# Strassen products for the up projections of two feed-forward blocks, and a down phase of its own

## The chip, the cores and the metric

The kernel runs on one core of one Trainium2 chip. The metric is the device time of one execution in microseconds. The engines are TensorE (PE, with its weight loads PEld), VectorE (DVE), ScalarE (ACT), GpSimd (POOL) and SyncE (SP), which here only issues transfers.

## The reference

Three blocks follow each other on x, 1024 tokens of 1024 channels. Block 2 and the first parts of blocks 1 and 3 (mixers and attention) are left alone. What the change touches are the feed-forward parts of blocks 1 and 3, with D_FF = 2816:

```python
h = rmsnorm(x, ffn_norm_g[l])
up = causal_depthwise_conv(h @ w_up[l], conv_w[l], conv_b[l])
a, bgate = jnp.split(up, [D_FF], axis=-1)
x = x + (jax.nn.silu(a) * bgate) @ w_down[l]
...
gate, up = jnp.split(h @ w_gate_up, 2, axis=-1)
return (jax.nn.silu(gate) * up) @ w_down
```

The convolution of block 1 is over three tokens, per channel. In block 3 the result is added to ALPHA times the residual, and a layer norm follows.

## The kernel before

Tiles hold 128 channels by 512 tokens; the tokens come as two halves. A matmul is made of three: each operand is split into a high part (rounded to float32r by ScalarE, line 324) and a low part (the rest, by GpSimd or VectorE, line 330), and high by high, high by low and low by high are summed in one PSUM bank (line 344). The function `split` writes this pair, and `w_load` does it for weights: a raw tile of 512 KB is loaded by SP (`w_dma`, line 359), and whi and wlo of 128 by 1024 are made of it. The weights of the whole program lie in one array, in the order of use, so a change of that order is a change in `_weights`.

The program is written as generators. The main one issues the matmuls and, right behind a product, what evicts it; side tasks are taken in between by a `Driver` that counts estimated time. What comes out is a fixed order on every engine, and semaphores between engines; each engine takes its own queue in order.

A feed-forward part (`ffn`) has 22 chunks (NFF). Chunk c is one tile of 128 gate channels (w = 0) and one of 128 value channels (w = 1): two weight tiles, two halves, eight k-tiles. Chunks 0 and 1 are done by `first_quad`, the others by `gemm_a` into banks named up; `evac` makes g of them, and `g_split` splits g into ghi and glo for the down product. After every second chunk `down` adds the products of two chunks of g with their rows of w_down to the 16 tiles X of the residual, in banks named dn. The last four chunks are added at the end.

In block 1, `evac` multiplies by the norm's row R into a tile u, and does the convolution on it: ScalarE's Identity with scale and bias, then two steps on VectorE, then Silu (w = 0) or the product with the gate (w = 1). The two tokens that the second half needs of the first are kept in a tile carry. In block 3, `evac` is Silu for w = 0 and a product for w = 1.

Of the kernel before, what the change touches and what calls it, by code (L numbers as in the profile page):

```python
# [39 lines left out]
def _weights(a):  # L40
# [9 lines left out]
    def ffn(up, down):  # L50
# [48 lines left out]


# [198 lines left out]
class Kernel:  # L299
    def __init__(self, tc, ins, outs, blocks=(1, 2, 3)):  # L300
        self.tc, self.nc, self.a, self.o = tc, tc.nc, ins, outs
        self.blocks = blocks
        self.drv = Driver()
        self.wn = 0
        self.wl, self.raws = [], []
        self.wi = self.wd = 0

# [35 lines left out]
    def mm(self, out, lhsT, rhs, start, stop):  # L343
        self.nc.tensor.matmul(out=out, lhsT=lhsT, rhs=rhs, start=start, stop=stop)  # L344
# [17 lines left out]

    def w_load(self):

        if self.wi >= self.a["wall"].shape[0]:
            return
# [20 lines left out]
    def w_retire(self, n):  # L387
        self.live -= n
        while len(self.wl) + self.live < 4 and self.wi < self.a["wall"].shape[0]:
            self.w_load()  # L390
# [110 lines left out]
    def build(self):  # L501
# [4 lines left out]
        with ExitStack() as ctx:  # L506
# [5 lines left out]
            self.hp = e(name="h", bufs=66)  # L512
# [10 lines left out]
            self.x2d = self.dp.tile([8, 128, S], F32, name="x2d")  # L523
            self.yd = self.dp.tile([8, 128, S], F32, name="yd")
# [16 lines left out]
    def first_quad(self, evac):  # L541

        ws = self.w_take(4)
        for half in range(2):
            self.drv.force(self.hs[half])
            pend = []
            for g in (0, 2):
                pss = [self.bank("fq") for _ in range(2)]
                yield from self.gemm_q(pss, ws[g:g + 2], half)
# [195 lines left out]
    def block1(self):  # L745
# [290 lines left out]
        def o_evac(j, half, ps):  # L1036
            self.tt(X[j][half], ps, X[j][half], ALU.add)
            sq = self.h("sq")
            self.act(sq, X[j][half], AF.Square)
            self.add_acc(accx, half, sq, nc.vector)  # L1040

        new_hs, new_rs = [None, None], [None, None]

        def done(half):
            new_hs[half] = drv.add(self.gen_split(half, lambda c: X[c][half],
                                                  lambda c: self.v("ffn_norm_g", c), H3), 500.0)
            new_rs[half] = drv.add(self.gen_rms(accx[half], half, D, 1e-6), 4800.0)
# [3 lines left out]
        self.H, self.hs, self.rs = H3, new_hs, new_rs  # L1051
# [10 lines left out]
        def evac(c, w, half, ps, up, G):  # L1062
            ch = c + NFF * w
            u = up.tile([128, HF + 2], F32, tag="u", bufs=4, name="u")
# [59 lines left out]
        yield from self.ffn(evac, add_last, done2, last)  # L1124
        self.H, self.hs, self.rs = H4, [iter(()), iter(())], rs

    def g_split(self, up, t, c):
        if c == NFF - 1:
            hi, lo = self.h("ghi", F32R), self.h("glo", F32R)
        else:  # L1130
            hi = up.tile([128, HF], F32R, tag="g", bufs=12, name="ghi")
            lo = up.tile([128, HF], F32R, tag="g", bufs=12, name="glo")
        self.split(hi, lo, t)
        return hi, lo

    def ffn(self, evac, add_last, done, by_half):

        X, G = self.X, {}
        with self.tc.tile_pool(name="ffn", bufs=4) as up:
            def down(i, ws, order, ev):  # L1140
                for j, half in order:
# [1017 lines left out]
```

## Time and profile before

| what | value |
|---|---|
| median of 3 runs | 3219.21 us (3215.55 to 3222.81) |
| profiled execution | 3218.23 us |
| its span, first to last instruction | 3216.4 us |
| mean granted TensorE clock | 0.966 |
| PE, DVE, ACT, POOL busy | 95%, 50%, 37%, 35% |
| HBM traffic | 161.06 MB read, 22.28 MB written |

The page counts an engine as busy while an instruction of its own runs; shares are means over parts of the program with different limits, so the same figures by stretch of time matter more. The feed-forward part of block 1 lies between about 445 and 1170 us of the span, that of block 3 between about 2440 and 3190.

### The profile page before, as it was taken

The numbers are of one execution on the slowest core, as the hardware profiler recorded it, in microseconds if no ns is written. First come the engines' busy times: TensorE is split into PE (matmuls) and PEld (weight loads), VectorE is DVE, ScalarE is ACT, GpSimd is POOL, SyncE is SP. The second block draws the span as 40 slices with busy tenths as digits, with TensorE's granted clock in tenths as the row PEclk, the third lists the DMA queues.
The fourth block names the chain that finished last, engine by engine and source line by source line (L and its number), as shares of the span: only waits on it lengthen the run. The fifth ranks groups of instructions, "written<-read, shape, count | busy, mean of one in ns | idle before, by whom it ended". The sixth has DMA issues, their size and how long they took to land.

```text
span 3216.4 us, 40756 instructions
## 1 busy us (share of the span) xinstructions
PE 3047.1 (95%) x15656; PEld 2592.4 (81%) x15656; DVE 1620.9 (50%) x3172; ACT 1179.0 (37%) x2276; POOL 1130.5 (35%) x899
## 2 busy tenths in 40 slices
PE   8999999999999989889998989988799999999997
PEld 7897788888888877868897779877688888888886
DVE  6443354444444469966646664666757112211216
ACT  4232232222222253566673356644435111111113
POOL 4314423333232365952214342234323323223321
PEclk9999999999999999989998989999799999999997
DMA  4101121111111112122113322100212111111111
GB/s 155 38 16 55 63 66 53 53 50 47 48 47 46 53 55 72 49 95 59 48 36 109 110 95 65 42 20 22 78 53 66 53 53 53 50 43 53 47 45 53
DMA packets 80306, 185.98 MB, mean 58 GB/s; under 512 B 15856, under 2 KB 27760, under 8 KB 80112
## 3 DMA queue, kind: packets, MB, share of 16 engines
q1 hardware_dynamic: 79824, 183.08, 17.7%
q8 instruction: 124, 2.03, 0.3%
q14 instruction: 70, 0.57, 0.1%
q10 hardware_dynamic: 288, 0.30, 0.0%
HBM read 161.06 MB, written 22.28 MB: 57 GB/s over the span
## 4 chain that ended last, share of the span: by engine, by line
PE 42%; DVE 8%; ACT 3%; issue 1%; DMA 0%; POOL 0%; ACTq 0%; DVEq 0%; SPq 0%; POOLq 0%
PE up L344 14%; PE dn L344 7%; PE op L344 5%; PE qk L344 3%; PE fq L344 2%; DVE f L1869 2%; PE o L344 2%; PE zp L344 1%; PE vp L344 1%; DVE pt L1885 1%; PE s L344 1%; PE sbo L344 1%; PE swo L344 1%; PE pt L1442 1%; PE ln L344 1%
## 5 line engine op out<-in xcount | busy, mean ns | idle before, releaser
L330 POOL TENSOR_TENSOR wlo<-raw,whi 128x1024 fp32r<-128x1024 f32 x240 | 580.2, 2435 | 720.0 <-ACT whi L324 704.3
L344 PE MATMUL up<-hlo,whi 128*128 128x512 f32 x1280 | 498.0, 389 | 0.0
L344 PE MATMUL up<-hhi,wlo 128*128 128x512 f32 x1280 | 498.0, 389 | 0.0
L344 PE MATMUL up<-hhi,whi 128*128 128x512 f32 x1280 | 497.9, 389 | 0.0
L324 ACT ACTIVATE whi<-raw 128x1024 fp32r<-128x1024 f32 x240 | 243.4, 1050 | 430.9 <-PE dn L344 292.2
L330 DVE TENSOR_TENSOR X<-dn,X 128x512 f32<-128x512 f32 (+1 forms) x328 | 219.4, 676 | 181.6 <-PE dn L344 181.4
L344 PE MATMUL dn<-ghi,whi 128*128 128x512 f32 (+1 forms) x736 | 283.0, 384 | 0.0
L344 PE MATMUL dn<-glo,whi 128*128 128x512 f32 (+1 forms) x736 | 282.4, 384 | 0.0
L344 PE MATMUL dn<-ghi,wlo 128*128 128x512 f32 (+1 forms) x736 | 282.2, 383 | 0.0
L344 PEld LDWEIGHTS up<-hlo,whi 128*128 128x128 f32 x1280 | 240.3, 188 | 50.0
L344 PEld LDWEIGHTS up<-hhi,whi 128*128 128x128 f32 x1280 | 240.3, 188 | 49.9
L344 PEld LDWEIGHTS up<-hhi,wlo 128*128 128x128 f32 x1280 | 240.3, 188 | 49.9
L330 DVE TENSOR_TENSOR gate<-up,gate 128x512 f32<-128x512 f32 x40 | 27.7, 692 | 406.7 <-PE up L344 406.7
L327 DVE SCALAR_TENSOR_TENSOR cv<-u,vec,cv 128x512 f32<-128x512 f32 x176 | 132.3, 752 | 138.0 <-ACT cv L324 61.1
L330 POOL TENSOR_TENSOR glo<-gate,ghi 128x512 fp32r<-128x512 f32 x44 | 56.9, 1292 | 335.3 <-ACT ghi L324 317.8
L344 PE MATMUL qk<-hhi,whi 128*128 128x512 f32 x384 | 163.3, 425 | 7.8 <-ACT hhi L324 7.1
L344 PEld LDWEIGHTS dn<-glo,whi 128*128 128x128 f32 x736 | 139.4, 189 | 28.3
L344 PEld LDWEIGHTS dn<-ghi,whi 128*128 128x128 f32 x736 | 139.4, 189 | 28.3
L344 PEld LDWEIGHTS dn<-ghi,wlo 128*128 128x128 f32 x736 | 139.3, 189 | 28.3
L344 PE MATMUL op<-hhi,wlo 128*128 128x512 f32 x384 | 154.2, 402 | 4.0 <-POOL wlo L330 4.0
L344 PE MATMUL op<-hhi,whi 128*128 128x512 f32 x384 | 156.3, 407 | 0.0
L344 PE MATMUL qk<-hlo,whi 128*128 128x512 f32 x384 | 154.5, 402 | 1.2 <-DVE hlo L327 1.2
(374 smaller groups left out, 6771.5 us busy)
## 6 DMA issues: line engine op xcount, KB each, us to landing
raw<-in_wall SPq DMA_DIRECT2D x240, 512.0 KB, 3.5
x2d<-X SPq DMA_DIRECT2D x32, 256.0 KB, 2.0
X<-x2d SPq DMA_DIRECT2D x32, 256.0 KB, 4.2
x<-in_xT SPq DMA_DIRECT2D x16, 256.0 KB, 5.9
X<-in_xT SPq DMA_DIRECT2D x16, 256.0 KB, 6.2
T<-in_rpbx SPq DMA_DIRECT2D x8, 448.0 KB, 3.9
yd<-ys SPq DMA_DIRECT2D x56, 64.0 KB, 1.6
c2d<-z SPq DMA_DIRECT2D x8, 256.0 KB, 4.3
```

Source lines behind the costliest of these rows:

```text
L324: self.nc.scalar.activation(out=out, in_=in_, func=func, bias=bias, scale=scale, **kw)
L327: self.nc.vector.scalar_tensor_tensor(out=out, in0=in0, scalar=s, in1=in1, op0=op0, op1=op1)
L330: (eng or self.nc.vector).tensor_tensor(out=out, in0=in0, in1=in1, op=op)
L344: self.nc.tensor.matmul(out=out, lhsT=lhsT, rhs=rhs, start=start, stop=stop)
L1442: nc.tensor.transpose(ps[:, 128 * b:128 * b + 128], pr[:, 128 * b:128 * b + 128], self.ident)
L1869: nc.vector.tensor_tensor_scan(out=rev, data0=rev, data1=rev, initial=carry, op0=ALU.mult, op1=ALU.bypass)
L1885: nc.vector.tensor_copy(out=pt[:, 0:w], in_=pst[:, 0:w])
```

## The change

Chunks 2 to 21 of both feed-forward parts are computed by seven products in place of eight. A chunk's weights are the two by two quarters A11, A12 (gate channels, first and second half of k) and A21, A22 (value channels), h the quarters B11 to B22 (k by half of the tokens). With S1 = A21 + A22, S2 = S1 - A11, S3 = A11 - A21, S4 = A12 - S2 and T1 = B12 - B11, T2 = B22 - T1, T3 = B22 - B12, T4 = B21 - T2, the products are P1 = A11 B11, P2 = A12 B21, P3 = S4 B22, P4 = A22 T4, P5 = S1 T1, P6 = S2 T2, P7 = S3 T3. They are summed in three banks named p1, p2 and p3 and in tiles e1, v1 and v2. In the code, X[c][0] and X[c][1] become the T in `gen_t`, once a block; `s_steps` gives six steps that make a chunk's S from its two raw tiles while the chunk before is multiplied, and `strassen` calls them between the products. A quarter is a pair shi, slo; A1 holds A11 and A12, S24 holds S2 and S4, as pairs whi, wlo.

For this, h is multiplied by the norm's row before it is split (`gen_h` in place of `gen_split` and `gen_rms`). X is overwritten by the T, so the residual goes to DRAM (x2d) before and comes back for the down phase; g goes to DRAM (gd) as it is made, and is loaded and split in a down phase after all chunks (`g_load`). The convolution's tile t lies in PSUM, the carry is copied by VectorE, and half of a chunk's evictions (`later`) are issued in the next chunk. The weights' order in the array follows.

```diff
-        u(0), u(1)
-        for i in range(1, NFF // 2 - 1):
-            u(2 * i)
-            out.extend([dn[2 * i - 2], dn[2 * i - 1]])
-            u(2 * i + 1)
-        u(NFF - 2), u(NFF - 1)
+        for c in range(NFF):
+            u(c)
+        out.extend(dn[:NFF - 4])
...
+S_TILES = ((36, 76), (178, 218))
...
-            self.hp = e(name="h", bufs=66)
+            self.hp = e(name="h", bufs=64)
...
-            self.tt(X[j][half], ps, X[j][half], ALU.add)
+            x = X[j][half]
+            self.tt(x, ps, x, ALU.add)
+            nc.sync.dma_start(out=self.x2d[j][:, HF * half:HF * half + HF], in_=x)
...
+            for c in range(8):
+                x = X[c][half]
+                hi, lo = self.h("hhi", F32R), self.h("hlo", F32R)
+                H3[0][c][half], H3[1][c][half] = hi, lo
+                self.stt(x, x, self.v("ffn_norm_g", c), row, ALU.mult, ALU.mult)
+                self.split(hi, lo, x, eng=nc.vector if c % 2 else None)
+                yield 0.0, 900.0
...
+        def put(c, w, half, ps, add):
+            u = UT[c, w, half] = self.up.tile([128, HF + 2], F32, tag="u", bufs=4, name="u")
+            if add is None:
+                self.act(u[:, 2:HF + 2], ps, AF.Copy)
+            else:
+                self.tt(u[:, 2:HF + 2], ps, add, ALU.add)
+        def conv(c, w, half):
+            ch, u = c + NFF * w, UT.pop((c, w, half))
             if half == 0:
-                nc.gpsimd.memset(u[:, 0:2], 0.0)
+                nc.vector.memset(u[:, 0:2], 0.0)
+                U[c, w] = self.small(2, "carry")
+                nc.vector.tensor_copy(out=U[c, w], in_=u[:, HF:HF + 2])
             else:
-                nc.gpsimd.tensor_copy(out=u[:, 0:2], in_=U.pop((c, w)))
-            self.tt(u[:, 2:HF + 2], ps, R[half], ALU.mult)
-            if half == 0:
-                U[c, w] = self.small(2, "carry")
-                nc.gpsimd.tensor_copy(out=U[c, w], in_=u[:, HF:HF + 2])
-            t = self.h("cv")
+                nc.vector.tensor_copy(out=u[:, 0:2], in_=U.pop((c, w)))
+            t = self.pt.tile([128, 512], F32, tag="t", name="t")
             self.act(t, u[:, 2:HF + 2], AF.Identity, bias=self.v("conv_b", ch), scale=self.v("conv_w2", ch))
             self.stt(t, u[:, 1:HF + 1], self.v("conv_w1", ch), t, ALU.mult, ALU.add)
             self.stt(t, u[:, 0:HF], self.v("conv_w0", ch), t, ALU.mult, ALU.add)
             if w == 0:
-                self.act(t, t, AF.Silu)
-                G[c, half] = t
+                A[c, half] = self.h("a")
+                self.act(A[c, half], t, AF.Silu)
             else:
-                self.tt(t, G[c, half], t, ALU.mult)
-                G[c, half] = self.g_split(up, t, c)
+                g = self.h("g")
+                self.tt(g, t, A.pop((c, half)), ALU.mult)
+                self.g_out(c, half, g)
+        def evac(c, w, half, ps):
+            put(c, w, half, ps, None)
+            conv(c, w, half)
...
+        def half(i, k, x):
+            T[i][0][k], T[i][1][k] = self.h("thi", F32R), self.h("tlo", F32R)
+            self.split(T[i][0][k], T[i][1][k], x, eng=P if k == 3 else V)
+        for k in range(4):
+            x11, x12 = X[k]
+            self.tt(x11, x12, x11, ALU.subtract)
+            half(1, k, x11)
+        yield
+        for k in range(4):
+            x11, x22 = X[k][0], X[k + 4][1]
+            self.tt(x11, x22, x11, ALU.subtract)
+            half(2, k, x11)
+        for k in range(4):
+            x12, x22 = X[k][1], X[k + 4][1]
+            self.tt(x12, x22, x12, ALU.subtract)
+            half(3, k, x12)
+        for k in range(4):
+            x11, x21 = X[k][0], X[k + 4][0]
+            self.tt(x21, x21, x11, ALU.subtract)
+            half(4, k, x21)
...
+        def quarter(src):
+            hi, lo = (self.up.tile([128, 512], F32R, tag="e", bufs=12, name=x) for x in ("shi", "slo"))
+            self.split(hi, lo, src)
+            return hi, lo
+        def whole(src):
+            hi = self.wp.tile([128, 1024], F32R, tag="whi", bufs=4, name="whi")
+            lo = self.wp.tile([128, 1024], F32R, tag="wlo", bufs=4, name="wlo")
+            self.split(hi, lo, src)
+            return hi, lo
+        L, R = slice(0, 512), slice(512, 1024)
+        ra = rb = None
+        def s0():
+            nonlocal ra, rb
+            ra, rb = self.raws[0:2]
+            self.raws = self.raws[2:]
+            self.wi += 2
+            st["A22"] = quarter(rb[:, R])
+        def s1():
+            self.tt(rb[:, R], rb[:, L], rb[:, R], ALU.add, P)
+            self.tt(rb[:, L], ra[:, L], rb[:, L], ALU.subtract, P)
+        def s2():
+            st["S1"] = quarter(rb[:, R])
+            st["S3"] = quarter(rb[:, L])
+        def s3():
+            st["A1"] = whole(ra)
+        def s4():
+            self.tt(ra[:, L], rb[:, R], ra[:, L], ALU.subtract, P)
+            self.tt(ra[:, R], ra[:, R], ra[:, L], ALU.subtract, P)
+        def s5():
+            st["S24"] = whole(ra)
+        return [s0, s1, s2, s3, s4, s5]
...
+            b1, b2, b3 = (self.bank(x) for x in ("p1", "p2", "p3"))
+            def p6():
+                yield from prod(b2, cur["S24"], 0, T[2], True)
+            def p1():
+                yield from prod(b1, cur["A1"], 0, B11, True)
+            if n == 0:
+                yield from p1()
+                yield from prod(b3, cur["S1"], 0, T[1], True)
+                yield from p6()
+            else:
+                yield from p6()
+                step()
+                yield from p1()
+            e1, v1 = self.h("e1"), self.h("v1")
+            self.act(e1, b1, AF.Copy)
+            self.tt(v1, b2, e1, ALU.add)
+            step()
+            for f in left[0]:
+                f()
+            if n > 0:
+                yield from prod(b3, cur["S1"], 0, T[1], True)
+            step()
+            yield from prod(b2, cur["S3"], 0, T[3], False)
+            v2 = self.h("v2")
+            self.tt(v2, b2, e1, ALU.add)
+            put(c, 1, 1, b3, v2)
+            step()
+            yield from prod(b1, cur["A1"], 512, B21, False)
+            put(c, 0, 0, b1, None)
+            for f in left[1]:
+                f()
+            step()
+            yield from prod(b2, cur["A22"], 0, T[4], False)
+            put(c, 1, 0, b2, e1)
+            for f in left[2]:
+                f()
+            step()
+            while steps:
+                step()
+            if n + 2 < n_all:
+                self.s_dma(n + 2)
+            elif n + 2 == n_all:
+                self.w_dma()
+                self.w_dma()
+            else:
+                tail()
+            yield from prod(b3, cur["S24"], 512, B22, False)
+            put(c, 0, 1, b3, v1)
+            left = later(c)
+            cur = nxt
...
+                if g == 0:
+                    for f in steps[0:3]:
+                        f()
...
+            def g_load(c, half, own):
+                x = self.h("gx")
+                nc.sync.dma_start(out=x, in_=self.gd[c][:, HF * half:HF * half + HF])
+                hi, lo = ((self.up.tile([128, 512], F32R, tag="e", bufs=12, name=y) if own else self.h(y, F32R))
+                          for y in ("ghi", "glo"))
+                self.split(hi, lo, x, eng=nc.vector if half else None)
+                G[c, half] = hi, lo
...
+            def tail():
+                del self.stops[0]
+                for a in g_group(0):
+                    g_load(*a)
+                for j in range(8):
                     for half in range(2):
-                        for w in range(2):
-                            ps = self.bank("up")
-                            yield from self.gemm_a(ps, ws[w], half)
-                            evac(c, w, half, ps, up, G)
-                    self.w_retire(2)
-                    if c == 2 * i and i < NFF // 2 - 1:
-                        ws = self.w_take(2)
-                        yield from down(i - 1, ws, every, add)
-                        self.w_retire(2)
+                        X[j][half] = self.h("X")
+                        nc.sync.dma_start(out=X[j][half], in_=self.x2d[j][:, HF * half:HF * half + HF])
+                self.w_load()
...
+        def put(c, w, half, ps, add):
+            if w and half:
+                B[c] = self.pt.tile([128, 512], F32, tag="t", name="t")
+                self.tt(B[c], ps, add, ALU.add)
+            elif w:
+                self.tt(ps, ps, add, ALU.add)
+                gate(c, 0, ps)
+            else:
+                a = A[c, half] = self.h("a")
+                if add is not None:
+                    self.tt(a, ps, add, ALU.add)
+                self.act(a, ps if add is None else a, AF.Silu)
+        def later(c):
+            return [lambda: gate(c, 1, B.pop(c))], [], []
```

How the order moves, at three places. First, ScalarE in block 1, one chunk before the change (cv is the convolution's tile, four for a chunk; the weights' high parts stand behind):

```order
L324 ACTIVATE cv<-u,vec 128x512
L324 ACTIVATE cv<-cv 128x512
L324 ACTIVATE cv<-u,vec 128x512
L324 ACTIVATE ghi<-cv 128x512
L324 ACTIVATE cv<-u,vec 128x512
L324 ACTIVATE cv<-cv 128x512
L324 ACTIVATE cv<-u,vec 128x512
L324 ACTIVATE ghi<-cv 128x512
L324 ACTIVATE whi<-raw 128x1024 x2
```

and one chunk after it, with buffer numbers (raw_4833 and raw_4831 are the next chunk's weights, u and a belong to this and the chunk before):

```order
L325 ACTIVATE shi_4864<-raw_4833 128x512
L325 ACTIVATE e1_4880<-p1_4849 128x512
L325 ACTIVATE t_4889<-u_4791,vec_76 128x512
L325 ACTIVATE a_4893<-t_4889 128x512
L325 ACTIVATE t_4896<-u_4847,vec_76 128x512
L325 ACTIVATE a_4900<-t_4896 128x512
L325 ACTIVATE shi_4914<-raw_4833 128x512
L325 ACTIVATE shi_4918<-raw_4833 128x512
L325 ACTIVATE whi_4938<-raw_4831 128x1024
L325 ACTIVATE u_4954<-p1_4849 128x512
L325 ACTIVATE t_4959<-u_4817,vec_76 128x512
L325 ACTIVATE whi_4990<-raw_4831 128x1024
```

Before, the weights' high parts are whole tiles after a chunk's evictions; now the next chunk's four high parts stand among evictions of two chunks, the last of them (S24) at the end. Second, PE at the seam from one chunk to the next, in the changed kernel:

```order
L346 MATMUL p3_4851<-hlo_3928,whi_4827 128x512
L346 MATMUL p3_4851<-hhi_3927,wlo_4828 128x512
L346 MATMUL p2_5013<-thi_4129,whi_4990 128x512
L346 MATMUL p2_5013<-tlo_4130,whi_4990 128x512
L346 MATMUL p2_5013<-thi_4129,wlo_4991 128x512
```

The first product of the new chunk (P6, into p2_5013) reads whi_4990 and wlo_4991, the pair that ScalarE's last row above begins. Third, VectorE where the T are made, in the changed kernel (X are the T before their split, thi and tlo the pair):

```order
L331 TENSOR_TENSOR tlo_4150<-X_3278,thi_4149 128x512
L331 TENSOR_TENSOR X_3280<-X_3559,X_3280 128x512
L331 TENSOR_TENSOR tlo_4155<-X_3280,thi_4154 128x512
L331 TENSOR_TENSOR X_3282<-X_3561,X_3282 128x512
L331 TENSOR_TENSOR tlo_4160<-X_3282,thi_4159 128x512
L331 TENSOR_TENSOR X_3284<-X_3615,X_3284 128x512
```

Nothing of this was there before. A subtraction and a low part follow each other, each low part behind its own high part on ScalarE; the evictions of the first quad's last tiles and v1 stand behind all of them.

## Rows read from the trace of the kernel before

**Rows 1.** The page, part 1: busy time and share by engine.

```profile
PE 3047.1 (95%) x15656; PEld 2592.4 (81%) x15656; DVE 1620.9 (50%) x3172; ACT 1179.0 (37%) x2276; POOL 1130.5 (35%) x899
```

**Rows 2.** Busy time by stretch; clock, DMA share and GB/s end the row.

```profile
core 0: us, PE busy (x) PEld busy (x) DVE busy (x) ACT busy (x) POOL busy (x), PEclk, DMA share, GB/s
560.00:640.00 80.00, 80.00 (x352) 65.72 (x351) 37.56 (x54) 22.54 (x29) 27.20 (x30) 1.00 0.17 53
...
2560.00:2640.00 80.00, 80.00 (x355) 66.26 (x353) 14.53 (x21) 14.47 (x19) 24.68 (x13) 1.00 0.14 42
```

**Rows 3.** Timeline of PE from 700 us: start, duration, instruction.

```profile
699.68 0.39 PE L344 MATMUL up<-hhi,whi 128*128 128x512 f32 x1
...
702.85 0.39 PE L344 MATMUL up<-hhi,wlo 128*128 128x512 f32 x1
```

**Rows 4.** Groups by line, 400 to 1200 us: busy, mean ns, idle before, releasers.

```profile
L330 POOL TENSOR_TENSOR wlo<-raw,whi 128x1024 fp32r<-128x1024 f32 x72 | 174.0, 2437 | 150.4 <-ACT whi L324 150.4
...
L327 DVE SCALAR_TENSOR_TENSOR cv<-u,vec,cv 128x512 f32<-128x512 f32 x176 | 132.3, 752 | 138.0 <-ACT cv L324 61.1 <-POOL u L1066 47.7 <-POOL u L1068 26.1
...
L324 ACT ACTIVATE cv<-u,vec 128x512 f32<-128x512 f32 x88 | 71.6, 814 | 128.8 <-DVE u L330 128.8
L324 ACT ACTIVATE whi<-raw 128x1024 fp32r<-128x1024 f32 x71 | 71.4, 1047 | 145.3 <-PE dn L344 133.9 <-PE op L344 4.5 <-issue 3.9
...
L330 POOL TENSOR_TENSOR glo<-cv,ghi 128x512 fp32r<-128x512 f32 x44 | 57.2, 1300 | 264.0 <-ACT ghi L324 264.0
L330 DVE TENSOR_TENSOR u<-up,R 128x512 f32<-128x512 f32 x80 | 55.2, 691 | 133.8 <-PE up L344 133.8
...
L330 DVE TENSOR_TENSOR cv<-cv 128x512 f32<-128x512 f32 x44 | 30.4, 692 | 1.5
...
L324 ACT ACTIVATE ghi<-cv 128x512 fp32r<-128x512 f32 x44 | 27.8, 633 | 105.6 <-DVE cv L330 105.6
L324 ACT ACTIVATE cv<-cv 128x512 f32<-128x512 f32 x44 | 27.8, 632 | 118.5 <-DVE cv L327 118.5
...
L324 ACT ACTIVATE R<-row 128x512 f32<-128x512 f32 x3 | 1.8, 598 | 6.7 <-PE row L449 6.7
```

**Rows 5.** DMA issues: count, size, median us from issue to landing.

```profile
raw<-in_wall SPq DMA_DIRECT2D x240, 512.0 KB, 3.5
...
X<-x2d SPq DMA_DIRECT2D x32, 256.0 KB, 4.2
```

**Rows 6.** Timeline, 699 to 706 us, of VectorE, ScalarE and GpSimd.

```profile
699.75 1.54 DVE L327 SCALAR_TENSOR_TENSOR cv<-u,vec,cv 128x512 f32<-128x512 f32 x2 [4.62 <-POOL u L1066]
...
701.32 0.63 ACT L324 ACTIVATE cv<-cv 128x512 f32<-128x512 f32 x1 [5.14 <-DVE cv L327]
...
705.14 0.63 ACT L324 ACTIVATE ghi<-cv 128x512 fp32r<-128x512 f32 x1 [2.40 <-DVE cv L330]
...
705.85 1.29 POOL L330 TENSOR_TENSOR glo<-cv,ghi 128x512 fp32r<-128x512 f32 x1 [3.71 <-ACT ghi L324]
```

**Rows 7.** Groups by line, 400 to 1200 us: the carry's copy.

```profile
L1072 POOL COPY carry<-u 128x2 f32<-128x2 f32 x44 | 8.2, 187 | 98.1 <-DVE u L330 98.1
```

**Rows 8.** Timeline, 435 to 439 us, of VectorE and GpSimd.

```profile
436.36 2.48 DVE L330 TENSOR_TENSOR sq<-sq 128x512 f32<-128x512 f32 x1 [0.74 <-ACT sq L324]
...
435.89 2.40 POOL L330 TENSOR_TENSOR wlo<-raw,whi 128x1024 fp32r<-128x1024 f32 x1 [4.96 <-ACT whi L324]
```

**Rows 9.** Timeline of PE: matmuls that ended a wait, in brackets.

```profile
252.85 0.50 PE L344 MATMUL u<-hhi,whi 128*128 128x512 f32 x1 [1.51 <-ACT whi L324]
...
255.28 0.80 PE L344 MATMUL u<-hhi,wlo 128*128 128x512 f32 x1 [1.70 <-POOL wlo L330]
...
1280.95 0.38 PE L344 MATMUL vp<-whi,hhi 128*128 128x256 f32 x1 [1.78 <-ACT whi L324]
1285.20 0.58 PE L344 MATMUL vp<-wlo,hhi 128*128 128x256 f32 x1 [3.86 <-POOL wlo L330]
```

**Rows 10.** Busy time by stretch, as in Rows 2, behind those waits.

```profile
255.10:258.50 3.40, 3.22 (x8) 2.54 (x9) 0.00 (x0) 0.00 (x0) 2.46 (x2) 0.50 0.51 159
...
1282.50:1289.30 6.80, 4.10 (x19) 4.10 (x20) 5.83 (x9) 4.69 (x8) 5.70 (x5) 0.50 0.24 80
```

More of the change, by code (lines that the diff above doesn't have):

```diff
@@ L341, in q_low, with mm @@
         return t
-    def mm(self, out, lhsT, rhs, start, stop):
-        self.nc.tensor.matmul(out=out, lhsT=lhsT, rhs=rhs, start=start, stop=stop)
+    def mm(self, out, lhsT, rhs, start, stop, more=False):
+        self.nc.tensor.matmul(out=out, lhsT=lhsT, rhs=rhs, start=start, stop=stop, skip_group_check=more)
     def split(self, hi, lo, src, scale=None, eng=None):
@@ L361, in w_dma, with w_more @@
             self.raws.append(raw)
+    def w_more(self):
+        return self.wi < (self.stops[0] if self.stops else self.a["wall"].shape[0])
     def w_load(self):
-        if self.wi >= self.a["wall"].shape[0]:
+        if not self.w_more():
             return
@@ L388, in w_retire @@
         self.live -= n
-        while len(self.wl) + self.live < 4 and self.wi < self.a["wall"].shape[0]:
+        while len(self.wl) + self.live < 4 and self.w_more():
             self.w_load()
@@ L548, in first_quad @@
                 pss = [self.bank("fq") for _ in range(2)]
-                yield from self.gemm_q(pss, ws[g:g + 2], half)
+                if half == 1 and early:
+                    early(g)
+                yield from self.gemm_q(pss, ws[g:g + 2], half, middle=middle if half == 1 and g else None)
                 pend += [(g + i, half, ps) for i, ps in enumerate(pss)]
@@ L1122, in done2 @@
             rs[half] = drv.add(gen_rr(half), 9000.0)
-        yield from self.ffn(evac, add_last, done2, last)
+        yield from self.ffn(evac, put, later, add_last, done2, last)
         self.H, self.hs, self.rs = H4, [iter(()), iter(())], rs
[L1127 to L1134, printed above, removed]
@@ new lines, in g_out, with gen_t @@
+    def g_out(self, c, half, g):
+        self.nc.sync.dma_start(out=self.gd[c][:, HF * half:HF * half + HF], in_=g)
+    def gen_t(self):
+        X, T = self.X, self.T
+        V, P = self.nc.vector, self.nc.gpsimd
+        def half(i, k, x):
[18 more added lines that the diff above has]
+            half(4, k, x21)
+        yield
@@ new lines, in s_dma, with strassen, prod @@
+    def s_dma(self, n):
+        pool = self.up if n % 2 else self.wp
+        for _ in range(2):
+            raw = pool.tile([128, 1024], F32, tag="raw", bufs=2, name="raw")
+            self.nc.sync.dma_start(out=raw, in_=self.a["wall"][self.wd])
+            self.wd += 1
+            self.raws.append(raw)
+    def strassen(self, put, later, tail):
+        hhi, hlo = self.H
+        B11, B21, B22 = (([hhi[k + o][x] for k in range(4)], [hlo[k + o][x] for k in range(4)])
+                         for o, x in ((0, 0), (4, 0), (4, 1)))
+        T = self.T
+        def prod(ps, w, off, b, start):
+            whi, wlo = w
+            for k in range(4):
+                c = slice(off + 128 * k, off + 128 * k + 128)
+                self.mm(ps, whi[:, c], b[0][k], start and k == 0, False, not start)
+                self.mm(ps, whi[:, c], b[1][k], False, False, not start)
+                self.mm(ps, wlo[:, c], b[0][k], False, k == 3, not start)
+                if k % 2:
+                    yield 6 * 216.0
+        n_all = NFF - 2
+        left = ([], [], [])
+        cur = self.s_first
+        for n in range(n_all):
+            c = n + 2
+            nxt, steps = {}, []
+            if n + 1 < n_all:
+                steps = self.s_steps(n + 1, nxt)
+            step = lambda: steps.pop(0)() if steps else None
+            b1, b2, b3 = (self.bank(x) for x in ("p1", "p2", "p3"))
[48 more added lines that the diff above has]
+            cur = nxt
+        for part in left:
+            for f in part:
+                f()
@@ L2083, in rest @@
                 def rest():
-                    self.act(x, x, AF.Identity, bias=ab[:, j:j + 1], scale=ALPHA)
+                    self.act(x, x, AF.Identity, bias=b)
+                    nc.sync.dma_start(out=self.x2d[j][:, HF * half:HF * half + HF], in_=x)
                 return low, rest
@@ L2134, in done2 @@
             seen[half] = []
-        yield from self.ffn(evac, add_last, done2, True)
+        yield from self.ffn(evac, put, later, add_last, done2, True, ALPHA)
 _OUT_SHAPE = (8, 128, S)
```

126 lines of the change are left out of this document (85 added, 41 removed).

## The prediction

> **What bounds the kernel now.** I read the page's busy shares first, then the stretches, then the groups of instructions by line. TensorE is busy 95% of the span [rows 1]. The windows say where it is the whole limit: in an 80 us stretch of either feed-forward block PE is busy 80.00 of 80.00 us at clock 1.00 [rows 2], while VectorE, ScalarE and GpSimd stand at a fifth to a half. In block 1's stretch GpSimd is at 27.2 of 80 us, ScalarE at 22.5. So PE's columns set the time there, and everything else hides behind them. What one matmul is worth is read from starts, not from the modelled 389 ns: 14 matmuls lie between the two starts shown, (702.85 - 699.68) / 14 = 0.227 us [rows 3].
>
> **What the change takes out.** A chunk is two weight tiles by two halves by eight k-tiles by three matmuls, 96. Seven quarter products of four k-tiles are 84. Twenty chunks in two blocks lose 12 each: 480 x 0.227 = **-108.8 us**, all on the path as PE has no idle time there. The down products keep their number. The rest of the change is work for the other three engines and waits for it.
>
> **What hides.** In the down phase a pair of chunks is 96 matmuls, 21.8 us. Against it stand two weight splits and four splits of reloaded g: GpSimd 2 x 2.44 + 2 x 1.30 = 7.5 us, ScalarE 2 x 1.05 + 4 x 0.63 = 4.6 us [rows 4], VectorE 16 adds of 0.69 and two low parts, 12.4 us. All fit. The traffic of g and X goes through SP's queue, whose loads land in 3.5 to 4.2 us [rows 5]. I cost these at nothing; were a load late, a pair would wait those 4 us.
>
> **Block 1's steady chunk.** PE would need 84 x 0.227 = 19.0 us. But the first product of a chunk (P6) reads S24, which is made while the chunk before runs, and the order puts its steps behind that chunk's evictions. ScalarE's queue holds, after e1, the two convolutions of half 0 and half 1 with their Silu, and only then the high parts of S1 and S3. So from the end of P1 the following ends last, with durations from [rows 4]:
> - e1 0.60, v1 on VectorE 0.69; two convolution steps 1.54, Silu 0.63; Identity 0.81, two steps 1.54, Silu 0.63: 6.4 us;
> - the high part of S1 0.63, then on GpSimd two quarter low parts and A1's whole low part, 1.30 + 1.30 + 2.44, then S2 and S4, 2 x 1.30: 8.3 us;
> - S24's high part 1.05 and low part 2.44: 3.5 us, and the third matmul of the next P6 can go.
>
> That is 18.2. Hand-overs between engines are 0.03 to 0.1 each [rows 6], about a dozen; the small copies below add some; instructions that follow on one engine overlap by as much. I take 18.6, bounds 17.6 and 19.6. PE then runs the other 22 matmuls of P6 and P1, 5.0 us, and its result is there 0.2 later: the loop closes at **23.8 us** a chunk. PE idles 4.8 of them, in two pieces, before P6 and before its third matmul. Nineteen chunks follow a first one: 19 x 4.8 = **+91 us** (bounds 72 and 110).
>
> The small copies of the carry move from GpSimd, where one takes 187 ns [rows 7], to VectorE. A VectorE instruction on SBUF can be held by GpSimd: the addition sq<-sq took 2.48 us and ended 0.55 us after the GpSimd split that had begun before it [rows 8]. No row read here has that copy on VectorE, so its price lies between 0.15 and one GpSimd instruction, 2.44. I take 0.2 for each of two on the loop, as GpSimd sits waiting for ScalarE when they come. The Trainium skill, "SBUF — State Buffer", section "Who interferes with whom", says that a VectorE copy can also take the port pair that it shares with GpSimd, and the later one blocks fully. By it, each of two copies a chunk could wait out a 1.30 us subtraction, 19 x 2.6 = 49 us more. The trace bears it out for a sum of two tiles, not yet for a copy of two columns.
>
> **The clock.** Where PE waited 1.51 and 1.70 us within 4 us, the granted clock was 0.50, 1.2 GHz, for the next 3.4 us; where it waited 1.78 and 3.86 us, for 6.8 us [rows 9, 10]. Block 1's two pieces add up between these pairs. The low stretch costs half its length, less what falls into the second wait (2.7 us in the second pair): 0.35 to 3.4 us a chunk. I take 1.3, nearer the first pair: **+25 us**.
>
> **The starts.** T1 to T4 are 16 tiles, each a subtraction, a high part on ScalarE and a low part. For 12 VectorE waits for the high part: 0.69 + 0.63 + 0.69 + 0.1 = 2.1, so 25.2; the four whose low part GpSimd makes cost 0.7 each: 28 us. Some are held as in [rows 8]; six by 1 us is an estimate, 6. In block 1 four evictions with convolution stand among them, 3.6 each, 14.4, and v1 behind: 49 us. PE meanwhile has some 54 matmuls of the first quad and P1, P5, P6 of the first chunk, 20 us. P7 then waits for v1 to have read its bank: about 29, and 5 for the row that now has to be there before the split and for A1: **+34** (20 to 45). Block 3 has no convolution, so 28 + 6 + 3 - 20 = 17, and 3 for A1: **+20** (10 to 28).
>
> **The turns to the down phase.** g and the first down weights are split on ScalarE after loads that SP issues behind the last g: 2 + 4.2 + 4.6, and low parts 3.7, less P3's 2.7: **+12** and, with shorter evictions, **+10**. Six long waits of starts and turns each bring a low clock, about 1.7: **+10**.
>
> **Block 3's steady chunk.** Here only gates stand before S1's split. What ends last starts at P4's end: add 0.69, gate 0.69, then SP, where the two raws of two chunks on stand behind the write of g. A single raw lands in 3.5 us [rows 5]; two at once between that and 7; I take 5.1. Then a high part 0.63, GpSimd's seven pieces of 1.30 and one of 2.44, 11.5, S24's high part 1.05, hand-overs 0.9 and the last low part 2.44: 23.1 in all. PE has P3, a chunk and two matmuls meanwhile, 98 x 0.227 = 22.2. Every second chunk waits about 1: **+9** (0 to 20).
>
> **The sum**: -108.8 + 91 + 25 + 34 + 20 + 12 + 10 + 10 + 9 = +102, on the profiled execution's 3218.2 us: **3320 us**, 3.2% slower. That execution lies 1.0 us under the median of the runs shown.
>
> **The rivals.**
> - Hidden preparation (0.10), the other side. If the loop from P1's end to the third matmul of P6 stayed under the five products and two matmuls that PE has meanwhile, 62 x 0.227 = 14.1 us, block 1 would not wait. It would take 4.5 us off my 18.6, what the convolutions hold ScalarE from S1's high part. For it: GpSimd's pieces of a chunk sum to 14.0 of 19.0 us, and no other engine has more. Against: an engine takes its queue in order, and the order shows that part behind both Silu. Then 91 + 25 fall away: 102 - 116 = -14, **3204 us**, faster.
> - A dearer clock (0.14). Every wait of block 1 brings the long stretch at 0.50, 3.4 us lost: 19 x 3.4 = 65 for 25, **3360 us**. For it: both pairs in [rows 10] brought a low clock. The Trainium skill, "TensorE: Matmul & The Clock Gate", section "HAM oscillation — how this bites in real kernels", has it so: bursts of matmuls that alternate with waits are slowed again after each one. By that rule each of the 19 chunks pays.
> - Late weights in block 3 (0.08): the second raw lands at 7, the chunk waits for it as GpSimd does nothing meanwhile, 2 us every second chunk more: +20, **3340 us**.
>
> **How the numbers follow.** My forecast has 0.66 and 0.02 is left for a partial hiding that ends level. Its own range: 91 down to 72, the clock to 7 and the two starts from 54 to 30 give 3259; upward 110, starts of 73 and the dearer clock reach 3398. I take 3245 to 3395, the low end 14 lower for turns and copies that cost nothing; the hidden case and the ends, 0.2 in all, stay outside. A measurement of this kernel tells 0.2% (6 us) from no change: faster 0.10, within 0.02, slower 0.88.
>
> **What would show it.** Right: PE's windows in block 1 at about 64 of 80 us, two waits of 2 to 3 us before P6 and its third matmul, ended by ScalarE's and GpSimd's parts of S24; clock under 1 there; a wait of 15 to 20 us before the first P7 that VectorE ends; block 3 near 19 to 20 us a chunk. Wrong: block 1 at 19 us a chunk, or the raw's landing as what ended its waits.

## The result and the profile after

The changed kernel takes 3359.97 us (median of 4 runs, 3358.95 to 3370.64) against 3217.93 for the kernel before: ratio 1.0447, 95% interval 1.0422 to 1.0472. Its profiled execution took 3359.32 us, span 3357.5, mean granted clock 0.939 where it was 0.966.

The page of the changed kernel, part 1, against [rows 1]: 480 matmuls and 24 us of PE's busy time are gone, and PE's share fell by five points, as the span grew by 141 us.

```profile
PE 3022.9 (90%) x15176; PEld 2537.3 (76%) x15176; DVE 1825.2 (54%) x3523; ACT 1299.8 (39%) x2494; POOL 1445.5 (43%) x1019
```

Busy time by stretch, changed kernel, columns as in [rows 2]. Block 1, full before, has 68 of 80 us now and a clock under 1; block 3 has 78 of 80.

```profile
640.00:720.00 80.00, 68.60 (x262) 53.55 (x261) 37.58 (x63) 26.66 (x40) 42.65 (x29) 0.88 0.18 63
720.00:800.00 80.00, 68.73 (x270) 53.92 (x269) 39.29 (x66) 27.31 (x41) 43.40 (x29) 0.91 0.18 60
...
2720.00:2800.00 80.00, 78.06 (x342) 63.65 (x341) 19.07 (x28) 22.95 (x32) 55.71 (x38) 1.00 0.23 79
```

One steady chunk of block 1, timeline of the changed kernel by engine (start, duration, instruction; in brackets the wait before it and who ended it).

```profile
773.61 0.60 ACT L325 ACTIVATE e<-p 128x512 f32<-128x512 f32 x1 [4.27 <-PE p L346]
774.11 0.78 ACT L325 ACTIVATE t<-u,vec 128x512 f32<-128x512 f32 x1
776.64 0.60 ACT L325 ACTIVATE a<-t 128x512 f32<-128x512 f32 x1 [1.76 <-DVE t L328]
777.14 0.78 ACT L325 ACTIVATE t<-u,vec 128x512 f32<-128x512 f32 x1
779.53 0.60 ACT L325 ACTIVATE a<-t 128x512 f32<-128x512 f32 x1 [1.62 <-DVE t L328]
780.03 1.14 ACT L325 ACTIVATE shi<-raw 128x512 fp32r<-128x512 f32 x2
...
788.40 1.06 ACT L325 ACTIVATE whi<-raw 128x1024 fp32r<-128x1024 f32 x1 [4.42 <-POOL raw L331]
...
780.73 2.55 POOL L331 TENSOR_TENSOR slo<-raw,shi 128x512 fp32r<-128x512 f32 x2 [7.31 <-ACT shi L325]
783.23 2.41 POOL L331 TENSOR_TENSOR wlo<-raw,whi 128x1024 fp32r<-128x1024 f32 x1
785.72 2.64 POOL L331 TENSOR_TENSOR raw<-raw 128x512 f32<-128x512 f32 x2
789.53 2.35 POOL L331 TENSOR_TENSOR wlo<-raw,whi 128x1024 fp32r<-128x1024 f32 x1 [1.17 <-ACT whi L325]
...
789.51 0.50 PE L346 MATMUL p<-thi,whi 128*128 128x512 f32 x1 [2.06 <-ACT whi L325]
...
791.94 0.80 PE L346 MATMUL p<-thi,wlo 128*128 128x512 f32 x1 [1.70 <-POOL wlo L331]
```

This is the loop of the prediction, piece by piece. P1 ends, e1 begins at 773.61; ScalarE goes through two convolutions with a Silu each, and S1's high part starts only at 780.03. GpSimd, idle for 7.31 us until then, makes two low parts, A1's, then S2 and S4; S24's high and low part follow. The third matmul of P6 goes 18.33 us after e1 began.

The granted clock behind the second wait, by windows of the changed kernel (PEclk is the third number from the end). The two stretches belong to two chunks in a row.

```profile
791.60:795.00 3.40, 3.06 (x7) 2.49 (x8) 0.00 (x0) 0.00 (x1) 0.28 (x1) 0.50 0.73 274
795.00:815.50 20.50, 18.24 (x78) 14.22 (x76) 12.85 (x21) 8.68 (x13) 12.25 (x9) 1.00 0.04 16
815.50:822.30 6.80, 5.30 (x13) 4.13 (x14) 0.00 (x0) 0.63 (x1) 2.73 (x2) 0.50 0.56 184
```

All 18 steady chunks have such a stretch at 1.2 GHz, short and long mostly in turn. PE works in it at half speed (matmuls start 0.43 us apart there, 0.23 elsewhere), so half of its busy time is lost: 1.5 and 2.65 us, 2.1 in the mean.

The other waits of the changed kernel, timeline by engine. The first P7 of block 1 waits 19.61 us, the first down product 9.31. At 1251 PE waits for VectorE, which waits for ScalarE, which waits for a load of g. In block 3 two writes of g, which wait for VectorE to make g, hold SP's queue for 10.53 us, and the raw loads go behind them.

```profile
542.72 0.80 PE L346 MATMUL p<-thi,shi 128*128 128x512 f32 x1 [19.61 <-DVE v L331]
...
1053.93 0.80 PE L346 MATMUL dn<-ghi,whi 128*128 128x512 f32 x1 [9.31 <-ACT whi L325]
...
1251.03 0.50 PE L346 MATMUL dn<-ghi,whi 128*128 128x512 f32 x1 [2.89 <-DVE X L331]
...
1249.13 1.25 DVE L331 TENSOR_TENSOR glo<-gx,ghi 128x512 fp32r<-128x512 f32 x1 [8.42 <-ACT ghi L325]
...
1247.85 4.57 ACT L325 ACTIVATE ghi<-gx 128x512 fp32r<-128x512 f32 x7 [9.44 <-DMA gx<-gd]
...
1239.97 2.69 SPq L361 DMA_DIRECT2D raw<-in_wall  x2
1242.72 4.14 SPq L1367 DMA_DIRECT2D gx<-gd  x8
...
2961.45 0.82 SPq L1254 DMA_DIRECT2D raw<-in_wall  x2
2969.80 10.53 SPq L1172 DMA_DIRECT2D gd<-g  x2
...
2967.33 0.63 ACT L325 ACTIVATE shi<-raw 128x512 fp32r<-128x512 f32 x1 [3.81 <-DMA raw<-in_wall]
...
2983.27 0.50 PE L346 MATMUL p<-thi,wlo 128*128 128x512 f32 x1 [1.64 <-POOL wlo L331]
```

Where the 141.1 us of span lie, between the first matmuls of the stages in both traces (each stage's matmuls at 0.227 us are taken off, so that the -108.8 stands apart; the forecast's 10 for the clock behind six waits is shared out, four waits to the starts, two to the turns):

| part | forecast | measured |
|---|---|---|
| 480 matmuls less | -108.8 | -108.8 |
| block 1, steady chunks with their clock | +91 +25 | +121 (18 chunks of 25.76 us) |
| starts of both blocks | +54 +6.7 | +78 (49 and 29) |
| turns and down phases | +22 +3.3 | +39 |
| block 3, steady chunks | +9 | +18 (19 chunks of 20.0 us) |
| block 2 and all before block 1's feed-forward | 0 | -6.6 |
| sum | +102 | +141 |

### The profile page after: what moved, and what is told of

Its sections match the earlier page's. It is cut to its first block, busy times and chain, and to the rows that moved or that the text cites. A ratio compares the mean times of both kernels' runs of the same rounds, so it can differ in the third digit from the quotient of the medians.

```text
span 3357.5 us, 41372 instructions
## 1 busy us (share of the span) xinstructions
PE 3022.9 (90%) x15176; PEld 2537.3 (76%) x15176; DVE 1825.2 (54%) x3523; ACT 1299.8 (39%) x2494; POOL 1445.5 (43%) x1019
## 5 line engine op out<-in xcount | busy, mean ns | idle before, releaser
L331 POOL TENSOR_TENSOR slo<-raw,shi 128x512 fp32r<-128x512 f32 x120 | 153.4, 1292 | 308.7 <-ACT shi L325 308.7
L346 PE MATMUL p<-thi,shi 128*128 128x512 f32 x480 | 190.3, 397 | 33.8 <-DVE v L331 33.8
L331 POOL TENSOR_TENSOR raw<-raw 128x512 f32<-128x512 f32 x160 | 207.0, 1294 | 12.6
L346 PE MATMUL p<-hhi,whi 128*128 128x512 f32 x480 | 191.9, 400 | 7.7 <-ACT whi L325 7.7
L346 PE MATMUL p<-hhi,wlo 128*128 128x512 f32 x480 | 189.9, 396 | 3.2 <-POOL wlo L331 3.2
L346 PE MATMUL p<-hlo,whi 128*128 128x512 f32 x480 | 190.5, 397 | 0.0
L346 PE MATMUL p<-tlo,shi 128*128 128x512 f32 x480 | 189.5, 395 | 0.0
L346 PE MATMUL p<-thi,slo 128*128 128x512 f32 x480 | 189.3, 394 | 0.0
L328 DVE SCALAR_TENSOR_TENSOR t<-u,vec,t 128x512 f32<-128x512 f32 x176 | 133.0, 756 | 66.9 <-ACT t L325 61.0
L331 POOL TENSOR_TENSOR beta<-beta,f 128x511 f32<-128x511 f32 (+3 forms) x96 | 88.5, 927 | 176.4 <-DVE beta L335 172.8
```

Source lines behind the costliest of these rows:

```text
L328: self.nc.vector.scalar_tensor_tensor(out=out, in0=in0, scalar=s, in1=in1, op0=op0, op1=op1)
L331: (eng or self.nc.vector).tensor_tensor(out=out, in0=in0, in1=in1, op=op)
```

## Experiments

Theories, lettered as in the expectations. A: in block 1 the chunk is a loop through ScalarE's queue order (S1's split behind both Silu), and the low clock follows from its waits. B: the raw loads, behind the writes of g on SP's queue, close a loop of their own, in block 3 and, nearly as long, in block 1. C: the sum of GpSimd's and VectorE's work is the bound, so that issuing earlier gains nothing. The ratios are against the kernel before on the same chip.

**e1_early_s**: the steps that split S1, S3 and A1 are issued before the convolutions left over from the chunk before.

```diff
             self.tt(v1, b2, e1, ALU.add)
             step()
+            if n > 0:
+                step()
+                step()
             for f in left[0]:
                 f()
...
```

> Edit: from the second chunk on, the steps that split S1, S3 and A1 are issued right behind e1 and v1, ahead of the convolutions left over from the chunk before; nothing else moves. Theory A (block 1's chunk of 25.8 us is set by S1's high part standing behind two Silu in ScalarE's queue, and by nothing else near it): the chunk falls to about 20 us, 18 x 5.5 = 100 us less than the changed kernel's 3360, about 3260. Rival B (the raw tiles, which SP issues behind the last write of g, close a loop of nearly the same length: P4's end to landing 9.3 us in the trace, then 16 us of ScalarE and GpSimd work, against 22.2 us of PE): chunks stay at 24.5 to 26 us, 3335 to 3365. Rival C (GpSimd's 14 us a chunk plus what VectorE holds it): also no gain. I expect B's number, as the landing ended ScalarE's wait for the first step already.

Measured: 3368.2 us, ratio 1.0461 (1.0440 to 1.0482). No gain, as B had it, 3 us over the top of its range. Timeline of this kernel:

```profile
738.81 5.54 SPq L1172 DMA_DIRECT2D gd<-g  x2
744.52 0.84 SPq L1254 DMA_DIRECT2D raw<-in_wall  x2
...
737.10 1.05 ACT L325 ACTIVATE whi<-raw 128x1024 fp32r<-128x1024 f32 x1
750.06 0.63 ACT L325 ACTIVATE shi<-raw 128x512 fp32r<-128x512 f32 x1 [11.91 <-DMA raw<-in_wall]
...
762.20 0.80 PE L346 MATMUL p<-thi,shi 128*128 128x512 f32 x1 [4.41 <-DVE v L331]
```

The two waits before P6 are gone, but one of 4.41 before P7 has come. ScalarE's first split of the next raw now waits 11.91 us for a load that SP issued at 744.52, behind two writes of g that held its queue for 5.54; e1 and the convolutions stand behind that split. A second loop, a little longer, lay under the first: from the first P6 behind the start to the first down product this kernel takes 502.6 us, the changed kernel 496.1.

**e5_raw**: only the raw loads are moved, from the chunk's end to its start, ahead of the writes of g.

```diff
+            if n + 2 < n_all:
+                self.s_dma(n + 2)
+            elif n + 2 == n_all:
+                self.w_dma()
+                self.w_dma()
             def p6():
...
-            if n + 2 < n_all:
-                self.s_dma(n + 2)
-            elif n + 2 == n_all:
...
+            if n + 2 > n_all:
                 tail()
```

> Edit: the two raw tiles of the chunk after next are issued at the start of a chunk, ahead of its writes of g, in place of near its end; the steps stay. Theory A: the loop over the two Silu is untouched, block 1's chunk stays at 25 to 26 us; block 3, whose waits of 0.6 to 1.6 us I put down to the raws' landing, loses them, 9 us, and the turns a little: 3335 to 3350. Rival B (the raws alone set block 1): block 1's chunk falls to about 20, 3250. Rival C: no change in block 1.

Measured: 3352.24 us, ratio 1.0411 (1.0390 to 1.0432). Block 3's window, and two matmuls of block 1, in this kernel:

```profile
2720.00:2800.00 80.00, 80.00 (x355) 66.27 (x354) 19.45 (x30) 22.36 (x33) 58.79 (x39) 1.00 0.24 82
```

```profile
769.84 0.50 PE L346 MATMUL p<-thi,whi 128*128 128x512 f32 x1 [2.06 <-ACT whi L325]
772.27 0.80 PE L346 MATMUL p<-thi,wlo 128*128 128x512 f32 x1 [1.70 <-POOL wlo L331]
```

Block 3's steady waits are gone, its chunks take 413 us where they took 427: the raws behind the write of g were their cause. The time fell by 8 us only, to 2 us over the top of the expected range; in this trace the stretch ahead of block 1's feed-forward part, which the edit does not touch, is 5 us longer. Block 1 keeps the two waits of the changed kernel to 0.01 us: the first loop decides there.

**e2_early_s_raw**: both edits.

> Edit: both of the above. Theory A with B as the second bound behind it: only now does block 1 go down, to 19.0 to 20.5 us a chunk, waits of P6 gone and the clock at 1.00 between: 18 x 5.5 = 100 and 10 in block 3, about 3250. Rival C (GpSimd's throughput): block 1 stays above 23 us, over 3300.

Measured: 3244.24 us, ratio 1.0074 (1.0059 to 1.0089). Windows of this kernel:

```profile
640.00:720.00 80.00, 79.39 (x343) 63.94 (x342) 59.10 (x86) 34.24 (x52) 56.17 (x37) 1.00 0.25 82
...
2640.00:2720.00 80.00, 80.00 (x355) 66.27 (x354) 20.36 (x30) 24.17 (x36) 57.98 (x40) 1.00 0.23 79
```

Undone alone, the first loop costs 8 us more and the second gives back 8; undone together they give back 116. Both blocks run close to PE's speed at clock 1.00 (a chunk of block 1 takes 19.7 us, its 84 matmuls alone 19.0), with GpSimd at 56 and VectorE at 59 of 80 us: theory C is out, GpSimd's and VectorE's work was not the bound.

**e3_fill**: the loops stay; in block 1, 8 spare matmuls are issued before P6 and 6 between its second and third. Their results are overwritten.

```diff
...
+                if left[1]:
+                    fill(b1, 8)
+                    yield from prod(b2, cur["S24"], 0, T[2], True, lambda: fill(b1, 6))
...
```

> Edit: only in block 1, 8 matmuls without use are issued before P6 and 6 between its second and third matmul, into P1's bank before P1 begins it; they read A1 and B11, which are there. PE has 14 x 0.227 = 3.2 us more to do a chunk, in the two waits of 2.1 and 1.7 us. Theory A with the clock as the prediction priced it: the waits are filled, the granted clock stays at 1.00, the 22 matmuls of P6 and P1 take 5.0 in place of 7.5 us, the chunk falls from 25.8 to 23.6: 18 x 2.2 = 40 us less, about 3320. Rival D (the clock costs nothing there, what lengthens the chunk is a longer chain on ScalarE, VectorE and GpSimd): unchanged or up to 10 us more than 3360.

Measured: 3331.78 us, ratio 1.0354 (1.0335 to 1.0373), 28 us under the changed kernel with 266 matmuls more (14 in each of 19 chunks); 40 were expected. Window, and the matmuls at P6, in this kernel:

```profile
640.00:720.00 80.00, 77.11 (x329) 61.16 (x329) 46.09 (x73) 29.87 (x46) 44.37 (x31) 1.00 0.17 60
```

```profile
727.41 0.50 PE L346 MATMUL p<-thi,whi 128*128 128x512 f32 x1 [1.17 <-ACT whi L325]
...
727.99 1.53 PE L346 MATMUL p<-hhi,whi 128*128 128x512 f32 x6
729.88 0.50 PE L346 MATMUL p<-thi,wlo 128*128 128x512 f32 x1 [0.36 <-POOL wlo L331]
```

The clock stays at 1.00, and a chunk takes 24.2 us ((824.28 - 630.58) / 8 between first matmuls of P6) where it took 25.76. PE still waits 1.17 and 0.36 us here, so its work is not the bound: this is the loop without the low clock, forecast at 23.8. The low clock adds some 1.6 us a chunk to it, since the slowed matmuls stand on the loop; D, by which the clock costs nothing, is out.

**e4_tpipe**: only the preparation of T1 to T4 is reordered, so that VectorE subtracts tile k + 1 while ScalarE makes the high part of tile k.

```diff
...
-            self.tt(x11, x12, x11, ALU.subtract)
-            half(1, k, x11)
...
+                self.tt(out, a, b, ALU.subtract)
+                if late is not None:
+                    half(i, late, of(late)[0])
+                late = k
...
```

> Only the order of the T tiles' pieces on VectorE is changed: the subtraction of tile k+1 is issued before the low part of tile k, so VectorE no longer waits for ScalarE's high part in between (1.42 us of waiting in a step of 2.05 us for one tile). Theory (the starts are a chain of VectorE pieces that wait for ScalarE): a tile costs VectorE 0.69 + 0.69 = 1.4 in place of 2.05, twelve tiles a block save about 8 us; the wait before the first P7 falls from 19.6 to about 11 in block 1 and from 14.2 to about 7 in block 3, and the time to 3340 to 3348. The steady chunks stay at 25.8 us. Rival (the start waits for the evictions with convolution that stand in the same queues, not for the T tiles): both waits stay within 2 us, 3358 to 3362.

Measured: 3344.59 us, ratio 1.0394 (1.0379 to 1.0410), 15 us under the changed kernel. The first P7 of block 1 in this kernel:

```profile
536.47 0.80 PE L346 MATMUL p<-thi,shi 128*128 128x512 f32 x1 [15.95 <-DVE v L331]
```

The time came out as expected, the wait fell only by half of what was expected: it is 15.95 in place of 19.61 (11 was expected), and 10.04 in block 3 (7 was). P7 itself goes 8.8 us earlier, counted from the first matmul of the feed-forward part (98.1 us in the changed kernel, 89.3 here), but PE reaches it 5.1 us earlier too: A1's split stands behind T1 in ScalarE's queue, and PE's wait for it fell from 6.40 to 3.93; the rest are shorter waits between that and P7. (The 1.42 us in the expectation are ScalarE's wait for VectorE in a step; VectorE's own wait is 0.76.)

**c1_all**: e2_early_s_raw and e4_tpipe together.

> The early steps and the early raw loads together with the reordered T tiles. Theory (loop and start are separate losses and add): e2_early_s_raw's time less the 15 us of the starts, 3225 to 3232, at or just above the kernel before. Rival (the first Strassen chunk's wait is only handed on to the next product, whose weights are split behind the T tiles on ScalarE): no more than 5 us gained, 3239 or more.

Measured: 3222.25 us, ratio 1.0013 (1.0003 to 1.0022), 22 us under e2_early_s_raw, 3 us under the low end of what was expected. Loops and starts are separate losses and add; why it is 22 us and not 15 was not taken apart.

**d1_ord**: c1_all, with chunk 2 done by eight products and A1 split before T1, so that the T tiles have a chunk more to hide behind.

```diff
...
+            if n < 1:
...
+                for w, half in ((0, 0), (0, 1), (1, 0), (1, 1)):
+                    ps = self.bank("pq")
+                    u, v = ((B11, B21), (B12, B22))[half]
+                    if w == 0:
+                        yield from prod(ps, cur["A1"], 0, u, True)
+                        yield from prod(ps, cur["A1"], 512, v, False)
+                    else:
+                        yield from prod(ps, cur["A21"], 0, u, True)
+                        yield from prod(ps, cur["A22"], 0, v, False)
...
```

> c1_all with chunk 2 of each block done by eight ordinary quarter products, so that Strassen begins with chunk 3, and with A1 split before the T tiles. It adds 2 x 12 matmuls, 5.4 us, and gives the T tiles 21.8 us of PE work more to hide behind. Theory (what the starts cost is the time of preparation not covered by PE work): the waits of 6.4 and 1.2 before the first up product go, and of the 19.6 and 14.2 before P7 together with the low clock after them some 25 us; 5.4 is paid. About 3205 (3195 to 3218), under the kernel before. Rival (the wait moves to the first P6, whose S24 now stands behind the T tiles and the evictions of one chunk more): 3225 or more.

Measured: 3203.95 us, ratio 0.9953 (0.9937 to 0.9969). The first P6 of block 1, and the matmul that waited behind it:

```profile
541.28 0.80 PE L346 MATMUL p<-thi,whi 128*128 128x512 f32 x1 [17.87 <-ACT whi L325]
543.72 0.79 PE L346 MATMUL p<-thi,wlo 128*128 128x512 f32 x1 [1.21 <-POOL wlo L331]
```

Both theories hold in part. The time is the first one's. But the wait did move to P6, whose S24 is split on ScalarE behind the T tiles, and it is 17.87 where c1_all waited 15.96 at P7, with PE 60 matmuls further on (96 of chunk 2 against 36 of P1, P5 and P6), 12 of them extra. Gone in block 1 are c1_all's waits of 3.92 and 1.70 us for A1, ahead of it, and of 2.37 and 1.70 at the P6 behind it. That the rest of the 18 us gained is the clock behind such waits is argued, not shown.

**d2_turn**: d1_ord, with loads of g and the first down weights prepared earlier, and later loads of g ahead of the weight loads on SP.

```diff
...
+            if n + 2 > n_all:
+                tail(0)
...
+                if i + 1 < len(rest):
+                    for a in rest[i + 1]:
+                        g_dma(*a)
                 self.w_retire(2)
...
```

> d1_ord with the turns to the down phase prepared earlier: the loads of the first four tiles of g and the splits of the first two down weights are issued behind e1 and v1 of the last chunk, their splits before its last product, and later loads of g stand ahead of the weight loads on SP. Theory (the turn waits for loads that SP issues late, and the late wait of the down phase, ended by VectorE, is a load of g held on SP's queue behind a weight load that waits for GpSimd): the waits of 9.7 and 1.2 and of 7.4 and 1.6 at the turns fall to under 3 each, those of 2.8 and 3.0 in the down phases go, and with the clock that comes back 15 to 25 us are gained: 3180 to 3192. Rival (the turn waits for the last chunk's g itself, or for the splits): under 8 us gained.

Measured: 3179.72 us, ratio 0.9879 (0.9865 to 0.9894): the fastest kernel here, 1.2% under the kernel before. The waits around the turn of block 1 that are left in this kernel:

```profile
921.86 0.50 PE L346 MATMUL dn<-glo,whi 128*128 128x512 f32 x1 [0.69 <-DVE glo L331]
...
934.52 0.80 PE L346 MATMUL dn<-ghi,whi 128*128 128x512 f32 x1 [5.79 <-DVE X L331]
```

The 9 us before the first down product are gone, and so are the late waits of both down phases: they were loads of g behind weight loads. A new one of 5.79 us has come in block 1 alone, for VectorE's additions to X; block 3 has none. VectorE's timeline in this kernel, 905 to 936 us, shows what they stand behind:

```profile
933.18 0.69 DVE L331 TENSOR_TENSOR g<-t,a 128x512 f32<-128x512 f32 x1
933.79 2.47 DVE L331 TENSOR_TENSOR X<-dn,X 128x512 f32<-128x512 f32 x4
```

The first additions follow without a pause on the last eviction with convolution of the last chunk. No run moved them.

## Why the prediction was right, and what was off

The direction and the mechanism were right, and the signs named ahead came: 68 us of 80 in block 1 for 64, waits of 2.06 and 1.70 us there for 2 to 3, 19.61 before P7 for 15 to 20, 20.0 us a chunk in block 3 for 19 to 20. Of the 39 us by which the span lies over the forecast the starts have 17, the turns 14, block 3's chunks 9 and block 1's chunks 5; block 2 and what lies ahead take 7 off.

**Block 1's loop** was forecast as 18.6 us from P1's end to the third matmul of P6, through ScalarE's queue; the timeline shows 18.33 from e1's start, with the pieces named, and e2_early_s_raw shows that moving the splits (with the raws) frees it. The hidden preparation (the rival on the other side) would have needed under 14.1; its own condition, S1's split ahead of the convolutions, is the first edit of e2_early_s_raw. That alone did not bring it (e1_early_s): the rival had overlooked that SP's queue closes a second loop of like length.

**The clock** was forecast at 1.3 us a chunk and 1.7 behind each of six long waits, +35. In block 1's steady chunks this was near. By e3_fill the loop without the low clock is 24.2 us, for 23.8, and the clock's share is 25.76 - 24.2 = 1.6 us a chunk, 28 us in 18 chunks, for 25. PE itself loses 2.1 us a chunk, but the slowed matmuls fill part of the loop, so that its waits are 2.06 + 1.70 = 3.8 us, not 4.8. Behind the starts and turns the clock was mis-sized. The windows below give PE's busy time in the low stretches of block 1's start and turn; half of it is (4.71 + 6.94 + 8.29) / 2 = 10 us for block 1 alone, where 3 waits at 1.7 were 5.

```profile
501.30:511.50 10.20, 4.71 (x10) 3.32 (x11) 5.21 (x7) 3.30 (x5) 5.25 (x3) 0.51 0.07 27
518.40:545.70 27.30, 6.94 (x13) 3.98 (x14) 15.86 (x24) 11.08 (x19) 8.48 (x7) 0.50 0.10 31
...
1047.00:1064.10 17.10, 8.29 (x18) 5.59 (x19) 9.97 (x15) 8.32 (x12) 7.21 (x4) 0.52 0.99 356
```

The measured time is the number of the rival with a dearer clock, 3360, but not by its sum, so that the rival's hit is luck: it had the long stretch and 3.4 us lost in each of 19 chunks, and PE lost 1.5 and 2.65 in turn. Half of its premise holds: none of the 18 chunks kept the full clock, but only about every second one has the long stretch. The Trainium skill, "TensorE: Matmul & The Clock Gate", section "HAM oscillation — how this bites in real kernels", says that bursts between waits are slowed each time. The trace agrees, and goes further: the page tells it of longer waits, for loads, and here the clock fell behind waits of 2.06 and 1.70 us.

**The starts**: the sum of the waits was near, its parts were not, and that they cancel is luck. For block 1, 29 us before P7 and 5 for the norm's row and A1 were forecast, 34. The long waits are 19.61 before P7, and 5.85 for the row, 6.40 and 1.21 for A1, 33 in all. What was put at 5 took 13.5: A1's split stands behind T1 on ScalarE (T1's high parts from 492.00 us, A1's at 504.49; with A1 first, in d1_ord, the waits for A1 are gone), so part of T1 is waited for ahead of the first product and not before P7. Block 3 has 14.18 for 17, and 1.31 and 1.95 for 3. What lies over the forecast in the table is the clock of the last paragraph, and some waits of 0.5 to 0.6 between matmuls of P6.

**What hides**: the loads of g were costed at nothing, with 4 us as the price if one were late. One was, in each block: 2.89 and 3.20 us and the clock behind them. The order shows why, and it was readable ahead: eight loads of g stand on SP behind two weight loads, which wait for GpSimd to free their buffers; d2_turn puts them ahead, and the waits go. The waits of SP's queue in the changed kernel, 1210 to 1252 us (total, times, longest):

```profile
SPq L361 <- POOL wlo L331: 38.7, 4, 17.7
```

**Block 3's steady chunks** cost 18 in place of 9. The place was right: with e5_raw the same count gives 5. The landing had been taken at 5.1 us, between 3.5 and 7; the rows show 5.88, from SP's issue at 2961.45 to ScalarE's start at 2967.33. The 18 lie between the forecast and the rival of late weights, which had 20 more.

**The carry's copies**: VectorE's two-column copy was priced at 0.2 where it stands on the loop. There it takes 0.16. Where GpSimd is at work it is held, off the loop (timeline of VectorE, changed kernel, the chunk shown above):

```profile
774.86 0.16 DVE L1105 COPY carry<-u 128x2 f32<-128x2 f32 x1
...
780.74 1.31 DVE L1105 COPY carry<-u 128x2 f32<-128x2 f32 x1
...
786.10 0.94 DVE L1107 COPY u<-carry 128x2 f32<-128x2 f32 x1
```

The 1.31 one ends at 782.05, where the first of GpSimd's two low parts from 780.73 ends too. So the trace agrees for two columns as well with the rule of the Trainium skill ("SBUF — State Buffer", section "Who interferes with whom"). The 49 us did not come, since GpSimd waits for ScalarE when the loop's copies run: it is idle from 773.42 to 780.73.

Block 2, which the change does not touch, is 5.6 us shorter in the changed kernel's trace, 1276.4 us for 1282.1. In the traces of the eight experiments, which do not touch it either, it takes 1277 to 1283 us. The two values lie at about the ends of that spread, so the change need not be the cause; what makes the spread is open.

## What to carry to other kernels

Fewer matmuls pay only if what prepares them keeps out of the queues that the products wait on: follow each engine's queue, DMA issues included, once around a whole iteration, and expect a second loop under the first. Undoing one of two loops of like length gained next to nothing here; undo both before a theory is dropped. Short repeated waits of PE cost their length and the clock behind it, and the clock's share can itself stand on the loop.

## What was not expected of the hardware

Adding work made the kernel faster: 14 spare matmuls in each of 19 chunks kept the granted clock at 1.00 in both windows of block 1 where it had been 0.88 and 0.91, and took 28 us off. The same two waits gave low stretches of 3.4 and 6.8 us, mostly in turn from chunk to chunk, so the chunks took about 25.2 and 26.1 us.
